# Entry of layer 0 of a two-layer diffusion backbone: unsplit modulation products, squares summed on TensorE, other weight order, two projections begun on half the features

## The chip, the cores and the metric

The kernel runs on one core of a Trainium2 chip. The core has five engines with queues of their own: TensorE (PE in the profile, its weight loads PEld), VectorE (DVE), ScalarE (ACT), GpSimd (POOL) and SyncE (SP), whose queue issues most transfers. TensorE reads on-chip memory (SBUF) and writes accumulators (PSUM). The metric is the device time of one execution in microseconds (us), as the median over runs.

## The reference, cut to what matters

One step of a two-layer backbone on 640 tokens (128 context, 512 latent) of 1024 features, all in 32-bit floats. Layer 0 runs gated linear attention beside latent attention, layer 1 differential attention; each is followed by a gated MLP. What the entry of layer 0 computes:

```python
s_ctx = silu(c_ctx)[None, :]; s_lat = silu(c)          # two conditioning vectors of 1024
mp = split(s_ctx @ w_ada[0] + b_ada[0], 6)             # context: shift, scale, gate, ...
ms = split(s_lat @ w_ada[0] + b_ada[0], 6)             # latent tokens
# rmsnorm(x, g) = x * rsqrt(mean(x * x) + 1e-6) * g ;  modulate(h, b, s) = h * (1 + s) + b
hp = modulate(rmsnorm(xp, norm_gain[0, 0]), mp[0], mp[1])
hs = modulate(rmsnorm(xs, norm_gain[0, 0]), ms[0], ms[1])
qa, ka, va, ga, lr_f, lr_b, cq, ckv, kr = split(h @ w_in)   # w_in: 1024 x 2144
```

## The kernel before

Activations lie with features on the 128 partitions (eight feature tiles, index k) and tokens along the rows, in two halves of 320 tokens (`CH`). To keep 32-bit accuracy with TensorE's faster format, an operand is split into a rounded part (hi, an ScalarE copy) and the rest (lo, a subtraction on VectorE or GpSimd), and three passes hi*hi, hi*lo, lo*hi stand for one product (`Weights.split`, lines 161 to 172; `proj`, lines 192 to 210). A product of unsplit 32-bit operands is issued as two slower passes.

The entry is lines 405 to 515. The two conditioning vectors go through SiLU (line 411). Of the modulation, only shift and scale of the first norm are needed at once: 2048 columns of `w_ada`, loaded as four groups of four quarters of 512 KB (line 419; quarters lie in turn in buffers `aw` and in the raw weight buffers `wraw`, four of each). `ada0(g)` multiplies group g: eight products, two per quarter, with the conditioning as the stationary operand of few columns and 512 columns of weights streaming. Quarter 1 of each group, and quarter 3 of group 3, are split first (hi on ScalarE, lo on GpSimd); the other eleven quarters are unsplit. The result is copied (line 438), transposed by TensorE (line 441) and given its bias. Groups 0 and 1 serve feature tiles 0 to 3, groups 2 and 3 tiles 4 to 7. Products and transposes take their accumulators in turn from the same two buffers (tag "p1").

`rms` (line 227) makes the norm factors of one half: it squares the eight tiles (ScalarE, lines 235 and 238), adds them up (VectorE, line 239), lets TensorE add over the partitions with a matrix of -1 (line 242) and takes the inverse root in a chain of ScalarE and VectorE steps (lines 244 to 250). The factors stay in a PSUM tile of tag "s". `apply_norm` (line 308) multiplies x by scale and factor (line 316), adds the shift (ScalarE, line 318) and splits into hi and lo: even tiles on VectorE (line 320), odd ones with a copy on ScalarE and a subtraction on GpSimd (lines 177 and 178). After groups 0 and 1 it runs tiles 0 to 3 of half 0, then of half 1; after groups 2 and 3 likewise tiles 4 to 7.

`ein(i)` loads, splits and multiplies block i of the input projection: 48 passes of 320 columns into one "s" tile. The blocks come in the order 0, 9, 10, 11, 12, 5, 6, 7, 8, 1, 2, 3, 4. Block 0 carries the low-rank decays, from which the decay products (`zmm`, line 504) are made right after block 9. Beside the blocks, VectorE works off the rest of the modulation of layer 0 as reductions against the conditioning (`Ada`, line 375, loads `araw`); these wait for the SiLU of line 479.

"s" tiles lie in two buffers, and each third one in a third buffer (`Ps.__call__`). In the entry the first two hold the factors of the halves, the third is block 0's and the fourth, in the buffer of the first, block 9's.

The order on each engine is not that of the text: a planner simulates the program with its own costs and places instructions by text order and readiness; after that each engine's queue runs strictly in the planned order. `tc.issue_after(i)` puts what is issued inside behind instruction i, but only on i's own engine.

Of the kernel before, what the change touches and what calls it, by code (L numbers as in the profile page):

```python
# [19 lines left out]
D = 1024  # L20
KT = 8
# [35 lines left out]
def build(tc, a):  # L57
# [169 lines left out]
    def rms(tp, bank, parts, denom, out=None, y=None, after=None, bufs=1):  # L227
# [7 lines left out]
        S.activation(out=acc, in_=parts[0], func=ACTF.Square)  # L235
        for s in parts[1:]:
            sq = sq_tile()
            S.activation(out=sq, in_=s, func=ACTF.Square)
            V.tensor_tensor(out=acc, in0=acc, in1=sq, op=ALU.add)  # L239
        o, q, y = bank[:, 0:n], sq_tile(), acc if y is None else y  # L240
        with tc.issue_after(after.ins) if after else ExitStack():
            PE.matmul(out=o, lhsT=negs, rhs=acc, start=True, stop=True)
# [65 lines left out]
    def apply_norm(tp, x, bc, hl, l, n, half, k0=0, k1=KT):  # L308
        c0, c1 = CH[half]
        for k in range(k0, k1):  # L310
            t = tp.tile([128, CUT], FP32, tag="nm_t", name="nm_t", bufs=3)[:, 0:c1 - c0]
            hi, lo = [z[:, k, c0:c1] for z in hl]
            for s0, s1, c in seg(c0, c1):
# [4 lines left out]
                S.activation(out=u if k % 2 else hi[:, r], in_=u, func=ACTF.Identity, bias=sh)  # L318
# [89 lines left out]
    csil = xp.tile([128, KT, 4], FP32, name="csil")  # L408
    csr = xp.tile([128, KT, 4], FP32R, name="csr")
    V.memset(csil, 0.0)  # L410
    tables(S.activation(out=csil[:, :, 0:2], in_=sm["cT"], func=ACTF.Silu))
    split(csil[:, :, 0:2], csr[:, :, 0:2], csr[:, :, 2:4])

    awp, awes = pool("aw", side="left")
    raws = []
    for g in range(4):
        for q in range(4):
            raws.append(W.tile("raw", [128, 2, 512], FP32) if q % 2 else awp.tile([128, 2, 512], FP32, tag="aw", name="aw", bufs=4))
            load = nc.sync.dma_start(out=raws[-1], in_=a["wada0a"][g, q])
        if g == 0:  # L420
            for q in range(4):
                nc.sync.dma_start(out=x[:, 2 * q:2 * q + 2], in_=a["xT"][:, 2 * q:2 * q + 2])

    def ada0(g):
        am = ps("p1", "adaps")
        for q in range(4):
            raw = raws[4 * g + q]
            if q % 2 == 0 or q == 3 and g < 3:
                for kk in range(2):
                    PE.matmul(out=am[0:4, :], lhsT=csil[:, 2 * q + kk], rhs=raw[:, kk], start=q == 0 and kk == 0, stop=q == 3 and kk == 1)  # L430
                continue
            w = W.split(raw, [128, 2, 512], G)
            for kk in range(2):
                k = 2 * q + kk
                PE.matmul(out=am[0:4, :], lhsT=csr[:, k], rhs=w[0][:, kk], start=False, stop=False)
# [932 lines left out]
```

## Time and profile before

| | |
|---|---|
| runs | 1793.81, 1790.93, 1793.09 us; median 1793.09 |
| profiled execution | 1789.83 us, span of its instructions 1788.1 us |
| TensorE busy | 1730.6 us (97%) |
| VectorE, ScalarE, GpSimd busy | 1256.9, 757.4, 310.0 us |
| mean granted TensorE clock | 0.989 of full speed |
| read from main memory | 166.59 MB |

Times in the rows are counted from the start of the span. The profile is of one execution, the median is over three others. TensorE's passes overlap, so a reported pass is longer than the distance to the next one, and the pace is read from starts. "<-" behind a wait names what ended it, as the profile infers it.

### The profile page before, as it was taken

What the parts mean: (1) busy time and instruction counts of PE and PEld (TensorE: products, weight loads), DVE (VectorE), ACT (ScalarE), POOL (GpSimd) and SP (SyncE); (2) the same over time, 40 slices, a digit from 0 to 9 for tenths busy, and PEclk for the clock granted to TensorE, in tenths of its full rate; (3) what the DMA queues carried; (4) which work ended last, traced back from release to release, by engine and by line L of the source; (5) the groups of instructions that cost most, each with busy time, mean ns of one, the idle gap of its engine ahead of it and who ended that gap; (6) DMA issues with size and microseconds to landing.
All of it is one profiled execution on the core that took longest, in us unless ns stands there. A gap on an engine that the chain in (4) does not pass through costs nothing. (4 is left out here: it accounts for less than half of the span.)

```text
span 1788.1 us, 29411 instructions
## 1 busy us (share of the span) xinstructions
PE 1730.6 (97%) x11716; PEld 1622.1 (91%) x11716; DVE 1256.9 (70%) x2398; ACT 757.4 (42%) x1354; POOL 310.0 (17%) x330
## 2 busy tenths in 40 slices
PE   6999999999999999999989999999999999999997
PEld 1898777889999999999988989898999999999996
DVE  4974877778799999945587777876575454545556
ACT  5454535544522232322366665665363232323233
POOL 3201021000310100000124243431041010101004
PEclk9999999999999999999999999998999999999998
DMA  9650002054356555522232111212122222222221
GB/s 359 211 178 10 29 1 74 4 186 133 95 177 200 166 178 179 163 65 89 63 117 73 34 59 36 72 50 72 59 83 83 71 79 75 71 83 71 60 83 60
DMA packets 57337, 176.59 MB, mean 99 GB/s; under 512 B 6064, under 2 KB 11568, under 8 KB 56816
## 3 DMA queue, kind: packets, MB, share of 16 engines
q1 hardware_dynamic: 53408, 160.59, 27.9%
q0 software_dynamic: 3792, 14.13, 2.3%
q8 instruction: 92, 1.51, 0.3%
q14 instruction: 45, 0.37, 0.1%
HBM read 166.59 MB, written 7.77 MB: 98 GB/s over the span
## 5 line engine op out<-in xcount | busy, mean ns | idle before, releaser
L207 PE MATMUL up<-B,whi 128*128 128x320 f32 x2560 | 479.2, 309 | 0.0
L163 ACT CAST whi<-wraw 128x1024 fp32r<-128x1024 f32 (+2 forms) x208 | 208.1, 1001 | 520.2 <-PE up L207 232.0
L207 PEld LDWEIGHTS up<-B,whi 128*128 128x128 f32 x2560 | 401.7, 188 | 0.0
L170 DVE TENSOR_TENSOR wlo<-wraw,whi 128x1024 fp32r<-128x1024 f32 (+2 forms) x175 | 205.0, 1172 | 226.5 <-ACT whi L163 226.5
L207 PE MATMUL up<-B,wlo 128*128 128x320 f32 x1280 | 291.4, 309 | 0.0
L207 PE MATMUL po<-A,whi 128*128 128x320 f32 x1312 | 246.3, 309 | 0.7 <-DVE u L980 0.5
L207 PEld LDWEIGHTS up<-B,wlo 128*128 128x128 f32 x1280 | 214.1, 188 | 0.0
L375 DVE CUSTOM_DVE_ANT_0 junk<-araw,cbc 128x1024 bf16<-128x1024 f32 x160 | 204.6, 1279 | 10.2 <-DMA araw<-in_wada0b 8.2
L178 POOL TENSOR_TENSOR A<-u,A 128x640 fp32r<-128x640 f32 x44 | 76.6, 1741 | 754.9 <-ACT A L177 729.9
L207 PEld LDWEIGHTS po<-A,whi 128*128 128x128 f32 x1312 | 205.8, 188 | 1.4 <-issue 0.7
L207 PE MATMUL po<-A,wlo 128*128 128x320 f32 x656 | 149.8, 309 | 0.5 <-DVE wlo L170 0.5
L216 PE MATMUL qko<-B,whi 128*128 128x320 f32 x512 | 118.6, 316 | 4.6 <-ACT B L318 1.6
L170 POOL TENSOR_TENSOR wlo<-wraw,whi 128x256 fp32r<-128x256 f32 (+1 forms) x117 | 97.5, 862 | 132.6 <-ACT whi L163 127.2
L352 PE MATMUL pot<-A,whi 128*128 128x320 f32 x512 | 114.0, 311 | 0.1
L207 PEld LDWEIGHTS po<-A,wlo 128*128 128x128 f32 x656 | 109.8, 188 | 0.8 <-DVE wlo L170 0.8
L978 DVE SCALAR_TENSOR_TENSOR u<-up,small,u 128x127 f32<-128x127 f32 (+1 forms) x176 | 95.5, 542 | 8.2 <-ACT u L976 7.4
L980 DVE SCALAR_TENSOR_TENSOR u<-up,small,u 128x127 f32<-128x127 f32 (+1 forms) x176 | 96.2, 548 | 4.5
L216 PEld LDWEIGHTS qko<-B,whi 128*128 128x128 f32 x512 | 86.7, 191 | 6.9 <-ACT B L318 1.9
L865 ACT ACTIVATE p<-sc,mn 128x768 f32<-128x768 f32 (+1 forms) x100 | 79.2, 796 | 31.2 <-DVE mn L864 30.5
L864 DVE TENSOR_REDUCE mn<-sc 128x1 f32<-128x768 f32 (+1 forms) x100 | 79.2, 816 | 13.7 <-PE sc L839 13.4
L352 PEld LDWEIGHTS pot<-A,whi 128*128 128x128 f32 x512 | 85.6, 188 | 1.4 <-issue 0.4
L334 DVE SCALAR_TENSOR_TENSOR x2t<-po,mod,x2t 128x128 f32<-128x128 f32 x88 | 44.2, 546 | 55.3 <-PE po L207 50.6
(296 smaller groups left out, 3048.7 us busy)
## 6 DMA issues: line engine op xcount, KB each, us to landing
wraw<-in_wup SPq DMA_DIRECT2D x88, 512.0 KB, 3.6
araw<-in_wada SPq DMA_DIRECT2D x48, 512.0 KB, 3.5
wraw<-in_wdn SPq DMA_DIRECT2D x40, 512.0 KB, 3.7
araw<-in_wada0b SPq DMA_DIRECT2D x32, 512.0 KB, 4.1
wraw<-in_wie SPq DMA_DIRECT2D x13, 512.0 KB, 4.3
aw<-in_wada0a SPq DMA_DIRECT2D x8, 512.0 KB, 9.3
wraw<-in_wada0a SPq DMA_DIRECT2D x8, 512.0 KB, 8.9
wraw<-in_woe SPq DMA_DIRECT2D x8, 512.0 KB, 4.3
```

What stands on the lines that cost most here:

```text
L163: S.copy(out=hi, in_=raw)
L170: eng.tensor_tensor(out=lo[:, z], in0=raw[:, z], in1=hi[:, z].bitcast(FP32), op=ALU.subtract)
L178: return (lo_eng or V).tensor_tensor(out=lo, in0=src, in1=hi.bitcast(FP32), op=ALU.subtract)
L207: PE.matmul(out=o, lhsT=w[wi][:, k], rhs=hl[ri][:, k, c0:c1], start=k == 0 and n == 0, stop=k == nk - 1 and n == 2)
L216: PE.matmul(out=o, lhsT=w[wi][:, k], rhs=hl[ri][:, k, c0:c1], start=k == 0 and n == 0, stop=k == nk - 1 and n == 2)
L334: V.scalar_tensor_tensor(out=x[:, k, s0:s1], in0=ps_ap[:, s0 - c0:s1 - c0], scalar=mods[l][:, g * KT + k, c:c + 1], in1=x[:, k, s0:s1], op ...
L352: PE.matmul(out=o, lhsT=ws[j + m][wi][:, k], rhs=hl[ri][:, k, c0:c1], start=k == 0 and n == 0, stop=k == nk - 1 and n == 2)
L375: V.tensor_tensor_reduce(out=junk, in0=raw, in1=self.cbc[:, j], op0=ALU.mult, op1=ALU.add, scale=1.0, scalar=0.0, accum_out=mods[l][:, t0 ...
L864: V.tensor_reduce(out=mn[:, m:m + 1], in_=ss[m][:, 0:nk], op=ALU.min, axis=AX.X)
L865: self.exp = S.activation(out=p[:, m, 0:nk], in_=ss[m][:, 0:nk], func=ACTF.Exp, scale=-1.0, bias=mn[:, m:m + 1], accum_out=li[:, m:m + 1])
L978: V.scalar_tensor_tensor(out=u[:, s0 + 1:s1], in0=r[:, s0:s1 - 1], scalar=cw[:, 0:1], in1=u[:, s0 + 1:s1], op0=ALU.mult, op1=ALU.add)
L980: last = V.scalar_tensor_tensor(out=u[:, s0:s1 - 1], in0=r[:, s0 + 1:s1], scalar=cw[:, 2:3], in1=u[:, s0:s1 - 1], op0=ALU.mult, op1=ALU.add)
```

## The change

All sixteen modulation quarters are multiplied unsplit, two columns of conditioning wide, and the zeroed and split copies of the conditioning go. `rms` gets a form (`pe=True`) in which TensorE sums the eight squared tiles itself, one product each; both halves' factors share one "s" tile. Groups 1 to 3 are queued on TensorE behind the last of these sums. The norm takes half 0 and half 1 of one feature tile together. The raw weights of block 0 are loaded ahead of group 3, those of blocks 9 and 10 behind it and ahead of the rotary tables and the conditioning. Blocks 0 and 9 are issued first for tiles 0 to 3, both, then for tiles 4 to 7 (`ein_part`). The SiLU of line 479 is queued on ScalarE behind the last step of the norm there.

```diff
--- before.py
+++ after.py
@@ -224,7 +224,7 @@
         with tc.issue_after(after.ins) if after else ExitStack():
             mark["tab"] = S.preload_act_table_set("natural_log_exp_and_others")
 
-    def rms(tp, bank, parts, denom, out=None, y=None, after=None, bufs=1):
+    def rms(tp, bank, parts, denom, out=None, y=None, after=None, bufs=1, pe=False):
 
         n = parts[0].shape[-1]
 
@@ -232,14 +232,18 @@
             return tp.tile([128, CUT], FP32, tag="rsq", name="rsq", bufs=2)[:, 0:n]
 
         acc = tp.tile([128, CUT], FP32, tag="racc", name="racc", bufs=bufs)[:, 0:n]
-        S.activation(out=acc, in_=parts[0], func=ACTF.Square)
-        for s in parts[1:]:
-            sq = sq_tile()
+        o = bank[:, 0:n]
+        for k, s in enumerate(parts):
+            sq = sq_tile() if k or pe else acc
             S.activation(out=sq, in_=s, func=ACTF.Square)
-            V.tensor_tensor(out=acc, in0=acc, in1=sq, op=ALU.add)
-        o, q, y = bank[:, 0:n], sq_tile(), acc if y is None else y
-        with tc.issue_after(after.ins) if after else ExitStack():
-            PE.matmul(out=o, lhsT=negs, rhs=acc, start=True, stop=True)
+            if pe:
+                mark["sum"] = PE.matmul(out=o, lhsT=negs, rhs=sq, start=k == 0, stop=k == len(parts) - 1)
+            elif k:
+                V.tensor_tensor(out=acc, in0=acc, in1=sq, op=ALU.add)
+        q, y = sq_tile(), acc if y is None else y
+        if not pe:
+            with tc.issue_after(after.ins) if after else ExitStack():
+                PE.matmul(out=o, lhsT=negs, rhs=acc, start=True, stop=True)
         with tc.issue_after(mark["tab"].ins):
             S.activation(out=q, in_=o, func=ACTF.Ln, scale=-1.0 / denom, bias=epst[:, 0:1])
             S.activation(out=y, in_=q, func=ACTF.Exp, scale=-0.5, bias=lnh[:, 0:1])
@@ -306,7 +310,7 @@
                          scale=gs[l][:, n, k, c:c + 1], bias=mods[l][:, 3 * n * KT + k, c:c + 1])
 
     def apply_norm(tp, x, bc, hl, l, n, half, k0=0, k1=KT):
-        c0, c1 = CH[half]
+        last, (c0, c1) = None, CH[half]
         for k in range(k0, k1):
             t = tp.tile([128, CUT], FP32, tag="nm_t", name="nm_t", bufs=3)[:, 0:c1 - c0]
             hi, lo = [z[:, k, c0:c1] for z in hl]
@@ -315,7 +319,7 @@
                 u, sh = t[:, r], mods[l][:, 3 * n * KT + k, c:c + 1]
                 V.scalar_tensor_tensor(out=u, in0=x[:, k, s0:s1], scalar=gs[l][:, n, k, c:c + 1], in1=bc[:, r],
                                        op0=ALU.mult, op1=ALU.mult)
-                S.activation(out=u if k % 2 else hi[:, r], in_=u, func=ACTF.Identity, bias=sh)
+                mark["norm"] = S.activation(out=u if k % 2 else hi[:, r], in_=u, func=ACTF.Identity, bias=sh)
                 if k % 2 == 0:
                     last = V.scalar_tensor_tensor(out=lo[:, r], in0=u, scalar=sh, in1=hi[:, r].bitcast(FP32),
                                                   op0=ALU.add, op1=ALU.subtract)
@@ -405,55 +409,49 @@
     misc = gg.tile([128, TOK], FP32, name="misc")
     xp, xes = pool("x0", side="right")
     x = xp.tile([128, KT, TOK], FP32, name="x0t")
-    csil = xp.tile([128, KT, 4], FP32, name="csil")
-    csr = xp.tile([128, KT, 4], FP32R, name="csr")
-    V.memset(csil, 0.0)
-    tables(S.activation(out=csil[:, :, 0:2], in_=sm["cT"], func=ACTF.Silu))
-    split(csil[:, :, 0:2], csr[:, :, 0:2], csr[:, :, 2:4])
+    csil = xp.tile([128, KT, 2], FP32, name="csil")
+    tables(S.activation(out=csil, in_=sm["cT"], func=ACTF.Silu))
 
     awp, awes = pool("aw", side="left")
-    raws = []
+    raws, pre = [], {}
     for g in range(4):
+        if g == 3:
+            pre[0] = W.raw(a["wie"][0], [128, KT, 128])
         for q in range(4):
             raws.append(W.tile("raw", [128, 2, 512], FP32) if q % 2 else awp.tile([128, 2, 512], FP32, tag="aw", name="aw", bufs=4))
-            load = nc.sync.dma_start(out=raws[-1], in_=a["wada0a"][g, q])
+            nc.sync.dma_start(out=raws[-1], in_=a["wada0a"][g, q])
         if g == 0:
             for q in range(4):
                 nc.sync.dma_start(out=x[:, 2 * q:2 * q + 2], in_=a["xT"][:, 2 * q:2 * q + 2])
+    for i in (9, 10):
+        pre[i] = W.raw(a["wie"][i], [128, KT, 128])
+    load = W.last_dma
 
     def ada0(g):
         am = ps("p1", "adaps")
         for q in range(4):
-            raw = raws[4 * g + q]
-            if q % 2 == 0 or q == 3 and g < 3:
-                for kk in range(2):
-                    PE.matmul(out=am[0:4, :], lhsT=csil[:, 2 * q + kk], rhs=raw[:, kk], start=q == 0 and kk == 0, stop=q == 3 and kk == 1)
-                continue
-            w = W.split(raw, [128, 2, 512], G)
             for kk in range(2):
-                k = 2 * q + kk
-                PE.matmul(out=am[0:4, :], lhsT=csr[:, k], rhs=w[0][:, kk], start=False, stop=False)
-                PE.matmul(out=am[0:2, :], lhsT=csr[:, k, 0:2], rhs=w[1][:, kk], start=False, stop=k == KT - 1)
-        ar = xp.tile([4, 512], FP32, tag="ar", name="ar", bufs=2)
-        V.tensor_copy(out=ar, in_=am[0:4, :])
+                PE.matmul(out=am[0:2, :], lhsT=csil[:, 2 * q + kk], rhs=raws[4 * g + q][:, kk], start=q == 0 and kk == 0, stop=q == 3 and kk == 1)
+        ar = xp.tile([2, 512], FP32, tag="ar", name="ar", bufs=2)
+        V.tensor_copy(out=ar, in_=am[0:2, :])
         at = ps("p1", "adat")
         for b in range(4):
-            PE.transpose(out=at[:, 4 * b:4 * b + 4], in_=ar[:, b * 128:(b + 1) * 128], identity=ident[0:4, 0:4])
+            PE.transpose(out=at[:, 2 * b:2 * b + 2], in_=ar[:, b * 128:(b + 1) * 128], identity=ident[0:2, 0:2])
         t0 = (g % 2) * 8 + (g // 2) * 4
-        av = at[:, 0:16].rearrange("p (t c) -> p t c", c=4)
-        add_b(0, t0, 4, av[:, :, 0:2])
-        m = mods[0][:, t0:t0 + 4]
-        V.tensor_tensor(out=m, in0=m, in1=av[:, :, 2:4], op=ALU.add)
+        add_b(0, t0, 4, at[:, 0:8].rearrange("p (t c) -> p t c", c=2))
         if g % 2:
             make_g(0, 0, (g // 2) * 4, (g // 2) * 4 + 4)
 
     ada0(0)
-    bcs = [rms(xp, ps("s", "rb")[:, 0:512], [x[:, k, c0:c1] for k in range(KT)], D, bufs=2) for c0, c1 in CH]
+    rb, last = ps("s", "rb"), None
+    bcs = [rms(xp, rb[:, 512 * h:512 * h + 512], [x[:, k, c0:c1] for k in range(KT)], D, bufs=2, pe=True) for h, (c0, c1) in enumerate(CH)]
     for g in range(1, 4):
-        ada0(g)
+        with tc.issue_after(mark["sum"].ins):
+            ada0(g)
         if g % 2:
-            for half in range(2):
-                last = apply_norm(xp, x, bcs[half], B, 0, 0, half, 2 * (g - 1), 2 * (g - 1) + 4)
+            for k in range(2 * (g - 1), 2 * (g - 1) + 4):
+                for half in range(2):
+                    last = apply_norm(xp, x, bcs[half], B, 0, 0, half, k, k + 1) or last
     xes.close()
     awes.close()
     scp, sces = pool("sc", side="left")
@@ -475,7 +473,7 @@
     adp.after = [last, load]
     with tc.issue_after(load.ins):
         adp.load(a["cbc"])
-    with tc.issue_after(last.ins):
+    with tc.issue_after(mark["norm"].ins):
         S.activation(out=adp.cbc, in_=adp.cbc, func=ACTF.Silu)
     cbd = drp.tile([128, 2, D], FP32, name="cbd")
     nc.gpsimd.dma_start(out=cbd, in_=adp.cbc)
@@ -483,7 +481,23 @@
         adp.group(0, 16 + 8 * c, [a["wada0b"][8 * c + i] for i in range(8)])
 
     def ein(i):
-        return proj(ps("s", "pe"), W(a["wie"][i], [128, KT, 128]), B, KT)
+        if i in begun:
+            return ein_part(i, KT // 2, KT)
+        w = W.split(pre.pop(i), [128, KT, 128]) if i in pre else W(a["wie"][i], [128, KT, 128])
+        return proj(ps("s", "pe"), w, B, KT)
+
+    begun = {}
+
+    def ein_part(i, k0, k1):
+        if k0 == 0:
+            begun[i] = (ps("s", "pe"), W.split(pre.pop(i), [128, KT, 128]))
+        pt, w = begun[i]
+        for k in range(k0, k1):
+            for n, (wi, ri) in enumerate(((0, 0), (0, 1), (1, 0))):
+                for c0, c1 in CH:
+                    PE.matmul(out=pt[:, P0 + c0:P0 + c1], lhsT=w[wi][:, k], rhs=B[ri][:, k, c0:c1],
+                              start=k == 0 and n == 0, stop=k == KT - 1 and n == 2)
+        return pt[:, P0:P0 + TOK]
 
     def rope(tp, z, t0=0):
         n, t1 = z.shape[0], t0 + z.shape[-1]
@@ -505,6 +519,8 @@
                       rhs=wdec[d * 32:d * 32 + 32, :], start=True, stop=True)
         return z
 
+    for i in (0, 9):
+        ein_part(i, 0, KT // 2)
     S.activation(out=misc, in_=ein(0), func=ACTF.Identity, bias=sm["miscb"][:, 0:1])
     nc.gpsimd.dma_start(out=kr[:, TOK:ALLK], in_=a["krc"])
     nc.gpsimd.dma_start(out=kr[64:128, 0:TOK], in_=misc[64:128, :])
```

## Rows read from the trace of the kernel before

**Rows 1.** The page's first part: busy us (share of the span) and instructions of each engine.

```profile
PE 1730.6 (97%) x11716; PEld 1622.1 (91%) x11716; DVE 1256.9 (70%) x2398; ACT 757.4 (42%) x1354; POOL 310.0 (17%) x330
```

**Rows 2.** Windows: stretch, length, busy us (instructions) by engine, TensorE clock, DMA share, GB/s.

```profile
60.00:70.00 10.00, 10.00 (x69) 9.48 (x68) 8.28 (x12) 3.88 (x5) 2.88 (x6) 1.00 0.63 189
```

**Rows 3.** Groups by line, TensorE, 54.4 to 65.5: xcount | busy, mean ns | idle before.

```profile
L207 PE MATMUL pe<-B,whi 128*128 128x320 f32 x47 | 8.9, 311 | 2.1 <-DVE nm_t L316 2.1
L207 PE MATMUL pe<-B,wlo 128*128 128x320 f32 x24 | 5.5, 309 | 0.0
```

**Rows 4.** Timeline of TensorE: start, duration, line, operation, count [idle before, releaser].

```profile
5.61 3.57 PE L430 MATMUL adaps<-aw,csil 128*4 128x512 f32 x4 [5.61 <-DMA aw<-in_wada0a]
...
22.73 0.40 PE L436 MATMUL adaps<-wlo,csr 128*2 128x512 f32 x1 [1.86 <-POOL wlo L170]
...
35.32 1.88 PE L430 MATMUL adaps<-wraw,csil 128*4 128x512 f32 x4
...
38.30 1.88 PE L430 MATMUL adaps<-aw,csil 128*4 128x512 f32 x4
...
43.40 0.40 PE L435 MATMUL adaps<-whi,csr 128*4 128x512 f32 x1
43.63 0.40 PE L436 MATMUL adaps<-wlo,csr 128*2 128x512 f32 x1
...
54.49 0.85 PE L207 MATMUL pe<-B,whi 128*128 128x320 f32 x4 [2.14 <-DVE nm_t L316]
...
65.09 0.70 PE L504 MATMUL z<-wdec,misc 32*128 32x256 f32 x4
...
73.59 0.85 PE L207 MATMUL pe<-B,whi 128*128 128x320 f32 x4
```

**Rows 5.** Timeline of TensorE's weight loads, one ahead of each pass.

```profile
12.49 0.09 PEld L430 LDWEIGHTS adaps<-aw,csil 128*4 128x4 f32 x1 [0.34 <-issue]
12.92 0.09 PEld L430 LDWEIGHTS adaps<-aw,csil 128*4 128x4 f32 x1 [0.34 <-issue]
```

**Rows 6.** Line 242 over the whole kernel: count: least/median/greatest ns, first to last start.

```profile
L242 PE MATMUL rb<-racc,negs x32: 432/433/537, 19.8 to 1777.5; 128*128 128x320 f32 x32
```

**Rows 7.** Timeline of TensorE in a later stage, unsplit products of 256 columns.

```profile
190.47 1.13 PE L620 MATMUL inc<-va,kdt 128*128 128x256 f32 x4
```

**Rows 8.** Timeline of VectorE (DVE).

```profile
25.89 2.37 DVE L239 TENSOR_TENSOR racc<-racc,rsq 128x320 f32<-128x320 f32 x1 [0.45 <-ACT rsq L238]
...
28.18 0.67 DVE L438 COPY ar<-adaps 4x512 f32<-4x512 f32 x1
...
30.23 1.84 DVE L316 SCALAR_TENSOR_TENSOR nm_t<-x0t,gs,rb 128x128 f32<-128x128 f32 x6
...
39.63 0.50 DVE L248 SCALAR_TENSOR_TENSOR rb<-rb,rsq 128x320 f32<-128x320 f32 x1 [0.85 <-ACT rsq L247]
...
48.28 1.84 DVE L316 SCALAR_TENSOR_TENSOR nm_t<-x0t,gs,rb 128x128 f32<-128x128 f32 x6
...
66.67 1.22 DVE L170 TENSOR_TENSOR wlo<-wraw,whi 128x1024 fp32r<-128x1024 f32 x1
```

**Rows 9.** Timeline of GpSimd (POOL).

```profile
25.56 2.35 POOL L170 TENSOR_TENSOR wlo<-wraw,whi 128x1024 fp32r<-128x1024 f32 x1 [2.89 <-ACT whi L163]
...
58.87 1.37 POOL L178 TENSOR_TENSOR B<-nm_t,B 128x320 fp32r<-128x320 f32 x1 [1.08 <-ACT B L177]
```

**Rows 10.** Timeline of ScalarE (ACT).

```profile
37.97 0.53 ACT L244 ACTIVATE rsq<-rb,scal 128x320 f32<-128x320 f32 x1 [1.93 <-PE rb L242]
...
40.91 1.91 ACT L479 ACTIVATE cbc<-cbc 128x2048 f32<-128x2048 f32 x1
```

**Rows 11.** Windows of 2 us; the clock is the third number from the end.

```profile
32.00:34.00 2.00, 2.00 (x5) 0.34 (x4) 1.50 (x6) 2.00 (x6) 0.67 (x1) 0.57 0.99 410
...
48.00:50.00 2.00, 2.00 (x9) 2.00 (x9) 1.96 (x7) 1.56 (x6) 0.22 (x1) 0.50 0.74 227
```

**Rows 12.** Waits of the SP queue, 0 to 66: total us, times, longest.

```profile
SPq L155 <- DVE wlo L170: 8.7, 2, 7.3
```

## The prediction

> **What bounds the kernel now.** I read the page's busy times first: TensorE is busy 97% of the span [rows 1], so time can only come from stretches where it stands still, runs at its lower clock, or does work that need not be done. The windows of 10 us came next: from 60 us on it is busy without a gap [rows 2], so what the entry hands over earlier moves the whole rest forward, and nothing in the entry counts except the moment from which TensorE streams the projections without a break. The timeline of TensorE gives that moment. The projections of blocks 0 and 9 need 96 passes of 320 columns; the groups by line count 71 of them after 54.4 us [rows 3], and the decay products behind them start at 65.09 [rows 4]. 54.49 to 65.09 is 10.6 us for some 72 passes, 0.147 us each: full pace. So 24 passes, the first half of block 0, came before, and TensorE stood 2.14 us ahead of 54.49. The releaser is VectorE's line 316, and that is no operand: the accumulator of block 9 is the fourth "s" tile, which reuses the one in which the norm factors of half 0 lie, and line 316 is their last reader. The number to predict is what replaces 65.09.
>
> **The sum.** Start: TensorE begins at 5.61 and its first four passes take 3.57 [rows 4]; a pass of 512 columns later takes 0.43 [rows 5], so a full-precision product of 512 columns (two passes) costs 0.86.
>
> Group 0 unsplit: eight products. The first two run at the slow pace (3.4 us), six take 5.2: done at 14.2. Before, its split quarter waited for ScalarE's cast and POOL's subtraction.
>
> Sums of squares: sixteen products of 128x320 replace fourteen VectorE additions and two products. A pass of this line is reported as 433 ns [rows 6]; the 512-column pass is reported about 0.16 longer than its pace, so the pace here is 0.27, a sum 0.54. From below: two passes overlapped wholly, 0.43; from above: four passes of 256 columns in 1.13 with 0.40 for the last [rows 7] pace at 0.243, which scales to 0.61. I take 0.54, the line's own row: 8.6 us (6.9 to 9.8). The squares go through two buffers, and one is also held by the factor chain of half 0 for 2.2 us (Ln at 37.97 to the product that ends at 40.13, [rows 8, 10]); meanwhile half 1 has one buffer, and a sum costs a square (0.5, like the Ln there) and a product one after the other, 1.0, instead of 0.54. Loss 0 to 1.6; I take 0.7. With 0.3 for the transposes of group 0, the last sum ends at 23.8 (21.4 to 26.2).
>
> Groups 1 to 3 are queued behind that sum on TensorE alone: 24 products, 48 passes of 0.43, 20.6 us. Between groups TensorE waits for the copy of the result, because two buffers carry both the products and their transposes: the last four passes of group 2 start at 35.32, group 3 at 38.30, which less 1.72 of streaming is 1.26 us [rows 4]. Two such gaps, 2.5; of a third, in front of the projections, 0 to 1.26, I take 0.8, since the first halves do not need it. First halves start at 47.7. Before, the last product of group 3 started at 43.63: the groups end later, not earlier.
>
> First halves of blocks 0 and 9: 48 passes, 7.0 us, to 54.8. Their accumulators are free, since both halves' factors now share one "s" tile.
>
> The norm of the other features runs meanwhile. From copy to first product took 28.18 to 30.23, 2.0 us [rows 8], so it starts at 48.9. Before it took from 48.28 to the end of the last POOL subtraction, 60.24 [rows 8, 9], with two weight subtractions of 1.2 in VectorE's queue; those weights now come before it, so 9.5 us: ready at 58.4. TensorE wants that last operand at 47.7+7.0+3x0.88+0.4=57.8. Stall 0.6, bounds 0 and 3.
>
> Second halves: 7.0 us. End 47.7+14.1+0.6=62.4. Gain 65.1-62.4=2.7 us. Cross-check: five quarters unsplit add 5x(1.72-0.92)=4.0 us of TensorE work (split passes follow at 0.23, [rows 4]) and fourteen sums 7.6. This 11.6 is paid out of waiting, such as 1.86 us for POOL ahead of 22.73.
>
> Edits at nothing. The SiLU of the layer's conditioning (1.91 and a table load ahead of it, [rows 10]) stood between the factors and the norm of half 1; it goes behind the norm, where only the VectorE reductions follow, and they start no earlier than the norm's end either way. Uncovered it costs these 1.91 and the load on VectorE, not on TensorE: VectorE's weight part at 66.67 is for the block that TensorE begins at 73.59 [rows 4, 8], 5.7 us of slack after its 1.2. Fewer VectorE additions, a smaller copy and no zeroing shorten queues that had slack. The weight loads moved ahead of the SP queue: block 0's load takes the buffer of a group-1 quarter and waits for TensorE until about 27 (23.8 and two quarters); block 10's takes block 0's buffer and waits for VectorE's subtraction (SP has waited 8.7 us for that already, [rows 12]). Queued behind it: the rotary tables, the conditioning and the reductions' loads. None is wanted before 55; a wait up to 50 is free, beyond it VectorE's reductions slip into the same 5.7 us.
>
> **One rule against the change.** VectorE's addition at 25.89 took 2.37 us beside a POOL subtraction of 2.35, an operation of that size otherwise 0.5 [rows 8, 9]. The Trainium skill, page "SBUF — State Buffer", section "Who interferes with whom", says that VectorE and GpSimd share one port pair as an exclusive lock, so that one of them stands still. By that rule the four POOL parts of the second norm would each stop VectorE; the norm would last about 12 us and the gain would be near nothing. The trace agrees at 25.89. My 9.5 us come from a stretch with the same POOL work, so such stops are partly in it already.
>
> **Rivals.**
> Fully packed: the planner puts first halves into the gaps between the groups, the sums lose nothing to the buffers and nothing stalls: 23.1+20.6+14.1=57.8, or 60.3 with the two gaps kept; gain 4.8 to 7.3, 1785.8 to 1788.3. For: the operands of the first halves come from group 1, ready long before. Against: such gaps stayed empty before.
>
> Norm still decides: groups end near 47, 3 us later than before, and the norm takes 12 us again because the weights' subtractions stay inside it: ready at 60.9, then the last feature of block 0 and block 9's second half (4.4): 65.3, gain about 0: 1793. For: it took that long before, and SP's wait can delay those weights. Against: VectorE and ScalarE have less to do.
>
> Slower by the clock: TensorE's granted clock was half, 1.2 GHz, in 32 to 34 and all of 48 to 50 [rows 11], after short waits and modest work. Unsplit products feed two weight columns and now make up most of the entry. Every 2 us at that clock lose 1. From 5.4 us of it the gain is gone, from about 13 it is slower by 0.2%; all three groups at 1.2 GHz would cost 20.6, or 1811. A few such spells: 1795 to 1800. Against: such products held full pace in 12 to 15 [rows 5]. The Trainium skill, page "TensorE: Matmul & The Clock Gate", Part 1, says the clock falls after idleness and comes back with activity; by that rule less idleness means fewer falls; the trace shows full pace right after the 2.14 us of waiting ahead of 54.49 [rows 3, 4], so it does not bear the rule out there.
>
> **How the numbers follow.** The profiled execution took 1789.83, span 1788.1 and 1.7 around it; that less 2.7 is 1787.1. It lies 3.3 under the median of the runs, 1793.09, against which I predict 1790.4. Forecast (gain 1 to 4.5; alone 1788.6 to 1792.1) 0.42; fully packed 0.25; norm decides 0.17; slower 0.16. A measurement of this kernel tells 0.2%, 3.6 us, from no change: faster 0.25 plus 0.16 of the forecast, 0.41; slower 0.14 (two parts in a hundred of that rival fall within); same the rest, 0.45. The range goes from 1785.5, the packed case with a little of the sums' cheap end, to 1797.0: every unknown at its dear end (26.2+20.6+2.5+1.3+14.1+3=67.7, 2.6 later than now) with 2.6 us at the lower clock.
>
> **What would show it.** Right: no POOL work before the norm; group 3's last pass near 46; projections from about 47.5 without a break; decay products near 62.4. The sums are wrong if group 1 starts outside 21 to 26; the cover is wrong if TensorE waits for line 316, 320 or 178 between the halves; the hand-over is wrong if the decay products move and the span does not. A clock row of 0.5 over the groups is the slow rival. All is wrong if TensorE still waits for the factors' tile.

## The result: 15 us slower

The changed kernel took 1807.07 us (median of 4 runs, 1806.36 to 1809.43) against 1792.01 for the kernel before: ratio 1.0087, 95% interval 1.0068 to 1.0107. The profiled execution took 1807.1, its span 1805.2. The page's busy line, in the columns of [rows 1]:

```profile
PE 1747.8 (97%) x11744; PEld 1630.5 (90%) x11744; DVE 1244.2 (69%) x2378; ACT 753.5 (42%) x1348; POOL 296.8 (16%) x325
```

VectorE, ScalarE and GpSimd have less to do, as the change meant, and TensorE 17.2 us more. The loss has a place: the decay products, the hand-over of [rows 4], start at 78.80 instead of 65.09, 13.7 later. From there to the first product of the next stage it is 88.2 us instead of 86.6, another 1.6. These two make 15.3 of the 17.1 us between the two profiled spans; the medians, of other executions, lie 15.1 apart. TensorE's timeline of the changed kernel, in the columns of [rows 4], shows the 13.7:

```profile
6.07 3.57 PE L434 MATMUL adaps<-aw,csil 128*2 128x512 f32 x4 [6.07 <-DMA aw<-in_wada0a]
...
15.73 1.34 PE L240 MATMUL rb<-rsq,negs 128*128 128x320 f32 x4
...
17.34 4.07 PE L240 MATMUL rb<-rsq,negs 128*128 128x320 f32 x12
24.50 6.66 PE L240 MATMUL rb<-rsq,negs 128*128 128x320 f32 x16 [3.09 <-DVE rb L254]
31.09 1.88 PE L434 MATMUL adaps<-aw,csil 128*2 128x512 f32 x4
...
39.22 1.88 PE L434 MATMUL adaps<-aw,csil 128*2 128x512 f32 x4
...
46.18 0.85 PE L498 MATMUL pe<-B,whi 128*128 128x320 f32 x4
...
50.25 1.88 PE L434 MATMUL adaps<-aw,csil 128*2 128x512 f32 x4
...
57.21 0.71 PE L498 MATMUL pe<-B,whi 128*128 128x320 f32 x3
...
61.08 0.41 PE L439 MATMUL adat<-small,ar 2*128 2x2 f32 x4
63.13 2.03 PE L498 MATMUL pe<-B,whi 128*128 128x320 f32 x7 [1.31 <-ACT B L322]
...
72.77 1.26 PE L498 MATMUL pe<-B,whi 128*128 128x320 f32 x4 [1.83 <-ACT B L177]
...
78.80 0.70 PE L518 MATMUL z<-wdec,misc 32*128 32x256 f32 x4 [2.44 <-DMA wdec<-in_wdec]
```

Read from the top: half 0's sums (L240) begin at 15.73; half 1's wait 3.09 us and end at 31.09, where group 1 begins; block 0's first half fills the gap in front of group 3 (46.18), which then starts at 50.25; block 9's first half (57.21 on) stands ahead of group 3's transposes (61.08), without which the norm of the other features cannot begin; then come a wait for a cast of the norm and one for the decay weights. VectorE (the norm, and the modulation's reductions, which came at 58.28 before):

```profile
61.92 1.72 DVE L320 SCALAR_TENSOR_TENSOR nm_t<-x0t,gs,rb 128x128 f32<-128x128 f32 x5
...
72.40 1.23 DVE L379 CUSTOM_DVE_ANT_0 junk<-araw,cbc 128x1024 bf16<-128x1024 f32 x1 [3.85 <-ACT cbc L477]
```

ScalarE at the end of that norm; the SiLU of the conditioning and its table load run ahead of the last cast, for the edit put them behind the last Identity (L322), not behind the last cast (L177):

```profile
68.58 0.56 ACT L322 ACTIVATE nm_t<-nm_t,mod 128x320 f32<-128x320 f32 x1
69.16 1.28 ACT L477 ACT_TABLE_LOAD   x1
70.45 1.91 ACT L477 ACTIVATE cbc<-cbc 128x2048 f32<-128x2048 f32 x1
72.27 0.44 ACT L177 CAST B<-nm_t 128x320 fp32r<-128x320 f32 x1
```

GpSimd, whose queue also issues the decay weights; the copy of the SiLU's result (L479) stands ahead of the norm's last subtraction (L178), and both ahead of that load (L467):

```profile
72.67 0.56 POOL L479 DMA_DIRECT2D cbd<-cbc  x1 [3.08 <-ACT cbc L477]
73.26 1.09 POOL L178 TENSOR_TENSOR B<-nm_t,B 128x320 fp32r<-128x320 f32 x1
74.30 0.55 POOL L467 DMA_DIRECT2D wdec<-in_wdec  x1
```

The 1.6 us behind the hand-over are a spell at 1.2 GHz. TensorE's windows of the changed kernel (length, busy, granted clock, DMA share, GB/s):

```profile
80.00:82.00 2.00, 2.00 (x10) 0.50 1.01 249
82.00:84.00 2.00, 2.00 (x11) 0.69 1.01 368
```

Windows of the kernel before behind its own decay products (66 to 72) showed the full clock. Ahead of the hand-over the lower clock makes no difference between the two: windows of 5 us there (length times 1 - granted clock) add up to some 3.4 us lost in either kernel.

### The profile page after: what moved, and what is told of

The parts are those of the page before. It is cut to its first block, busy times and chain, and to the rows that moved or that the text cites. A ratio compares the mean times of both kernels' runs of the same rounds, so it can differ in the third digit from the quotient of the medians.

```text
span 1805.2 us, 29419 instructions
## 1 busy us (share of the span) xinstructions
PE 1747.8 (97%) x11744; PEld 1630.5 (90%) x11744; DVE 1244.2 (69%) x2378; ACT 753.5 (42%) x1348; POOL 296.8 (16%) x325
## 5 line engine op out<-in xcount | busy, mean ns | idle before, releaser
L163 ACT CAST whi<-wraw 128x1024 fp32r<-128x1024 f32 (+2 forms) x203 | 202.9, 1001 | 523.4 <-PE up L207 231.4
L178 POOL TENSOR_TENSOR A<-u,A 128x640 fp32r<-128x640 f32 x44 | 76.2, 1732 | 756.9 <-ACT A L177 731.9
L170 POOL TENSOR_TENSOR wlo<-wraw,whi 128x256 fp32r<-128x256 f32 x112 | 85.8, 797 | 106.0 <-ACT whi L163 106.0
L880 DVE TENSOR_REDUCE mn<-sc 128x1 f32<-128x768 f32 (+1 forms) x100 | 79.2, 816 | 15.5 <-PE sc L855 15.1
L338 DVE SCALAR_TENSOR_TENSOR x2t<-po,mod,x2t 128x128 f32<-128x128 f32 x88 | 44.2, 546 | 55.3 <-PE po L207 50.6
```

Source lines behind the costliest of these rows:

```text
L163: S.copy(out=hi, in_=raw)
L170: eng.tensor_tensor(out=lo[:, z], in0=raw[:, z], in1=hi[:, z].bitcast(FP32), op=ALU.subtract)
L178: return (lo_eng or V).tensor_tensor(out=lo, in0=src, in1=hi.bitcast(FP32), op=ALU.subtract)
L880: V.tensor_reduce(out=mn[:, m:m + 1], in_=ss[m][:, 0:nk], op=ALU.min, axis=AX.X)
```

## The experiments

"Hand-over" is the start of the first decay product in the profiled execution, which is one of the runs. The median of the kernel before was 1790.07 to 1791.2 beside e1 to e15, and ratios are against its runs on the same chip. The entry itself began earlier in the profiled executions of e1 to e5 and e10 than in the changed kernel's (first sum at 15.0, 14.1, 14.5, 14.2, 14.5 and 14.7 instead of 15.73, same instructions before it), so 0.7 to 1.6 us of a gain in hand-over are not the edit's.

| kernel | hand-over | median us (runs) | ratio (95%) |
|---|---|---|---|
| before | 65.1 | 1792.01 (4) | 1 |
| changed | 78.8 | 1807.07 (4) | 1.0087 (1.0068 to 1.0107) |
| e1 sums before chains | 72.9 | 1804.94 (4) | 1.0084 (1.0062 to 1.0106) |
| e2 transposes first | 73.4 | 1803.91 (4) | 1.0077 (1.0062 to 1.0092) |
| e3 SiLU last | 73.2 | 1800.15 (4) | 1.0058 (1.0043 to 1.0073) |
| e4 decay weights early | 74.7 | 1809.74 (4) | 1.0102 (1.0085 to 1.0119) |
| e5 all four | 66.1 | 1797.0 (10) | 1.0033 (1.0016 to 1.0050) |
| e6 e5, products split | 66.8 | 1800.58 (5) | 1.0050 (1.0032 to 1.0068) |
| e7 e2 to e4, VectorE sums | 61.2 | 1791.42 (10) | 1.0002 (0.9978 to 1.0025) |
| e8 e7, products split | 69.3 | 1799.05 (9) | 1.0035 (1.0016 to 1.0054) |
| e9 e7, SiLU in the norm | 62.6 | 1792.99 (12) | 1.0001 (0.9990 to 1.0012) |
| e10 changed, SiLU in the norm | 74.1 | 1803.53 (6) | 1.0063 (1.0047 to 1.0080) |
| e11 before, unsplit products | 65.6 | 1791.76 (11) | 0.9996 (0.9985 to 1.0007) |
| e12 changed, VectorE sums | 67.7 | 1798.75 (9) | 1.0039 (1.0026 to 1.0052) |
| e14 e9, block 0 first | 63.5 | 1792.3 (12) | 1.0004 (0.9990 to 1.0017) |
| e15 e14, weights late | 63.2 | 1790.89 (12) | 1.0006 (0.9991 to 1.0020) |

**One wait each.** Theory A: the loss is four waits that the order makes, each removable by order alone. Theory B: it is the added TensorE work.

e1 takes both halves' sums before either factor chain:

```diff
-    bcs = [rms(xp, rb[...], [...], D, bufs=2, pe=True) for h, (c0, c1) in enumerate(CH)]
+    for ph in ("sums", "chain"):      # rms does only its sums, or only its chain
+        bcs = [rms(xp, rb[...], [...], D, bufs=2, pe=ph) for h, (c0, c1) in enumerate(CH)]
```

> The changed kernel with one edit: the sums of squares of both halves are issued ahead of either half's factor chain, so that half 1's sums have no write of VectorE in the shared tile to wait for. Theory A (the loss is waits that the new order makes, each of which can be taken out by itself): the wait of 3.1 us for line 254 goes and the second eight sums run at about 0.6 us each; group 1 starts at 25 to 26.5 instead of 31.1, the decay products start near 73.5 instead of 78.8, time about 1802. Theory B (the loss is TensorE work added, 4.0 us of unsplit products and 7.6 of sums, and waits only sit where slack is left): group 1 starts earlier but the wait comes back in front of the second halves; decay products at 77.5 or later, time 1806 to 1808.

TensorE's timeline of e1:

```profile
16.62 9.54 PE L240 MATMUL rb<-rsq,negs 128*128 128x320 f32 x28
...
72.94 1.22 PE L521 MATMUL z<-wdec,misc 32*128 32x256 f32 x4 [2.50 <-DMA wdec<-in_wdec]
```

The wait is gone, group 1 starts at 26.1 instead of 31.1, the hand-over comes 5.9 earlier, 5.1 of it the edit's. The median fell by 2.1 only, less than either number of theory A. And 28 passes take 9.5 us, 0.34 each, at the full clock. ScalarE's timeline of e1 says why: two squares, then a wait for TensorE to free their two buffers, every 1.37 us.

```profile
20.19 1.01 ACT L238 ACTIVATE rsq<-x0t 128x320 f32<-128x320 f32 x2 [0.36 <-PE rb L240]
21.56 1.01 ACT L238 ACTIVATE rsq<-x0t 128x320 f32<-128x320 f32 x2 [0.35 <-PE rb L240]
```

e2 queues block 9's first half behind group 3's transposes:

```diff
-    for i in (0, 9):
-        ein_part(i, 0, KT // 2)
+    ein_part(0, 0, KT // 2)
+    with tc.issue_after(mark["adat"].ins):     # the last transpose
+        ein_part(9, 0, KT // 2)
```

> The changed kernel with one edit: the first half of block 9 is queued on TensorE behind the transposes of group 3. Theory A: the scale and shift of tiles 4 to 7 are ready 3.5 us earlier (norm starts near 58.3 instead of 61.9), the decay products start 3 to 3.7 us earlier, near 75.5, time about 1803.5. Theory B: the norm starts earlier but TensorE has the passes of block 9 still to do and ends no earlier than 78; time 1806 to 1808.

TensorE's timeline of e2: the last transposes come 5.2 earlier, 3.6 of it the edit's, the decay products 5.4 (3.7), though they now wait longer for their weights. That is theory A's outcome, and so is the median of 1803.91.

```profile
55.87 0.41 PE L439 MATMUL adat<-small,ar 2*128 2x2 f32 x4
...
73.45 0.77 PE L518 MATMUL z<-wdec,misc 32*128 32x256 f32 x4 [3.11 <-DMA wdec<-in_wdec]
```

e3 puts the SiLU behind the last cast:

```diff
-    with tc.issue_after(mark["norm"].ins):
+    with tc.issue_after(mark["cast"].ins):     # S.copy in split()
```

> The changed kernel with one edit: the SiLU of the conditioning is queued behind the last cast of the norm instead of behind its last shift. Theory A: the last cast runs at 69.1 instead of 72.3, the wait of 1.8 us for it goes, and the load of the decay weights behind it on the POOL queue moves too; decay products near 76, time about 1804. Theory B: no more than 1 us; time 1806 to 1808.

ScalarE's timeline of e3 has the order that was meant; the hand-over comes 5.6 earlier, 4.3 of it the edit's: more than theory A's 2.8 and than the 3.2 us of the SiLU and its load, since its copy on GpSimd's queue now stands behind the last subtraction and the decay weights too. The norm of tiles 4 to 7, first multiplication to last subtraction, takes 8.7 us instead of 12.4.

```profile
67.83 0.46 ACT L177 CAST B<-nm_t 128x320 fp32r<-128x320 f32 x1
68.31 1.28 ACT L477 ACT_TABLE_LOAD   x1
```

e4 issues the decay weights on SP's queue:

```diff
-    nc.gpsimd.dma_start(out=wdec, in_=a["wdec"])
     with tc.issue_after(load.ins):
+        nc.sync.dma_start(out=wdec, in_=a["wdec"])
```

> The changed kernel with one edit: the decay weights are loaded from the SP queue right behind the entry's loads, not from the POOL queue behind the norm's subtractions. Theory A: the wait of 2.4 us ahead of the decay products goes, they start at 76.4 instead of 78.8; time about 1804.5. Theory B: the wait moves to the next block, whose weight part VectorE subtracts at 76.6 to 77.8; time 1806 to 1808.

The hand-over comes 4.1 earlier (2.6 of it the edit's) and the total does not follow; it is past both theories. TensorE's waits in e4, 78 to 175 us (total, times, longest), show a new one, for the instruction with which VectorE reads decay products out of their accumulator (L544), while its reductions still begin late. From the hand-over to the next stage e4 needs 92.5 us, 4.3 more than the changed kernel.

```profile
PE pe L207 <- DVE ab L544: 3.4, 1, 3.4
```

e5 has all four edits.

> The changed kernel with the four edits together (sums of both halves first, block 9 behind group 3's transposes, SiLU behind the last cast, decay weights on SP's queue). Theory A (waits made by the order are the loss, and they add up): decay products near 63 to 65 instead of 78.8, as in the kernel before (65.1), time within 3 us of it. Theory C (TensorE's hand-over is no longer the bound: VectorE's reductions, which start behind the SiLU, now lag behind the blocks): decay products near 64 but a wait for VectorE later in the blocks gives back 3 to 6 us; time 1795 to 1798.

The four gains, 21.0 added up, are 15.8 without the earlier entry, and come to 11.4 together (12.7 less 1.3): they lay partly beside each other. The hand-over is back at 66.1, so B falls as an account of the whole 13.7: all the added work is still there. It is not back below 65.1 either, and the time (1797.0) is theory C's, not A's, though TensorE's only wait for VectorE's reading of decay products is gone.

**Which part costs what.** e6 splits the quarters again on top of e5; e7 takes e2 to e4 and lets VectorE add the squares again, without queueing the groups behind the sums; e8 is e7 with the quarters split.

```diff
-    bcs = [rms(xp, rb[...], [...], D, bufs=2, pe=True) for h, (c0, c1) in enumerate(CH)]
+    bcs = [rms(xp, rb[...], [...], D, bufs=2) for h, (c0, c1) in enumerate(CH)]
     for g in range(1, 4):
-        with tc.issue_after(mark["sum"].ins):
-            ada0(g)
+        ada0(g)
```

> The four repairs, and the five modulation quarters split again as in the kernel before. Theory D (with the waits out, what is left is TensorE work, and unsplit products cost 4.0 us of it): decay products 3 to 4 us earlier than with the four repairs alone. Rival (the splits bring back their own waits for ScalarE and POOL, 1.6 to 1.9 us each): within 1 us of it.

> The repairs that apply, with the squares added up by VectorE again and the groups no longer queued behind the sums; products stay unsplit. Theory D: fourteen sums less on TensorE are worth 7 to 9 us; decay products 55 to 58 unless the norm of tiles 4 to 7 binds at about 60. Rival: VectorE's additions delay the copies and the factors, decay products within 2 us of those of the four repairs.

> Split products and VectorE's sums as in the kernel before, with the rest of the change (shared factor tile, weight order, halves of blocks 0 and 9) and the repairs that apply. Theory D: least TensorE work of the four kernels, decay products at 56 to 60, time 1783 to 1788 if nothing behind binds. Rival (theory C): decay products there, but VectorE's reductions bind behind them, time 1788 to 1793.

VectorE's sums are worth 4.9 us of hand-over and 5.6 of the median (e5 to e7), less than theory D's 7 to 9. So theory B holds for a part: with the four waits gone, some 5 us of the loss are left, and they go when TensorE no longer makes the sums. Splitting the quarters again saves nothing, against theory D: it costs 0.7 (e5 to e6) or 8.1 (e7 to e8), the latter where VectorE has the sums as well; for e8 theory D had forecast the earliest hand-over of all, and its rival too. TensorE's timelines of e7, then e8, show where these two part, at the product that completes half 1's sum (L246):

```profile
27.36 0.81 PE L246 MATMUL rb<-racc,negs 128*128 128x320 f32 x2 [0.79 <-DVE racc L242]
```

```profile
37.60 0.81 PE L246 MATMUL rb<-racc,negs 128*128 128x320 f32 x2
```

In e8 it stands behind group 2's split products, though VectorE's last addition ended at 30.4; the norm of tiles 4 to 7 then ends at 65.3 instead of 57.2. In e7's profiled execution, a long one of 1802.67 us, the lead of 3.9 is lost before the next stage, at a wait for VectorE and to the lower clock (5.1 us); TensorE's timeline of e7:

```profile
61.18 1.13 PE L517 MATMUL z<-wdec,misc 32*128 32x256 f32 x4 [2.13 <-ACT misc L524]
...
120.99 1.44 PE L207 MATMUL pe<-B,whi 128*128 128x320 f32 x4 [3.27 <-DVE ab L544]
```

e9 is e7 with the SiLU's own edit undone, e10 the changed kernel with that alone undone, e11 the kernel before with unsplit quarters alone, e12 the changed kernel with VectorE's sums alone (the diff shown for e7).

```diff
-    with tc.issue_after(mark["norm"].ins):     # e7: mark["cast"]
+    with tc.issue_after(last.ins):
```

> The kernel of e7 (VectorE's sums, unsplit products, block 9's half behind the transposes, the decay weights early), but the SiLU of the conditioning stands where it stood before, between the norm factors and the norm of the second half. Theory C (VectorE's reductions bind behind the hand-over because the late SiLU lets them begin late): decay products at 61 to 63, the reductions begin before 59 and end near 118 instead of 124.8, TensorE's 3.3 us for VectorE's ab is gone, 1784 to 1788. Theory D (the reductions are held by their own loads, 11.0 us of idle time in e7): an early SiLU doesn't help, the wait for ab stays, the SiLU and its table load cost up to 3.2 us in the norm, decay products at 63 to 65, 1792 to 1796.

> The changed kernel with one edit undone: the SiLU of the conditioning back between the norm factors and the second half of the norm. Theory A (the moved SiLU delayed the last casts and, over its copy to memory, POOL's queue with the decay weights): both waits go, decay products from 78.8 to 72 to 74, some 1799 to 1801. Theory B (its 1.9 us and the table load then stand in the norm, which sets the end here): decay products at 75 to 77, 1802 to 1805.

> The kernel before with one part of the change alone: the five split quarters of the modulation products are unsplit. Theory A (the split's casts and subtractions held VectorE, POOL and TensorE more than the 4.0 us of added TensorE work): the wait of 1.86 us for POOL ahead of group 1 goes and the norm's engines are freer, decay products at 62 to 64, 1787 to 1789.5. Theory B (added passes stand in front of the groups, and the block 9 accumulator still waits for the norm's last reader): decay products at 64.5 to 66, 1790 to 1793.

> The changed kernel with one edit undone: the squares are summed on VectorE again, and groups 1 to 3 are not queued behind the sums. Theory A (the sums on TensorE cost their passes and the wait of 3.1 us for half 0's factors): the hand-over comes 5 to 8 us earlier, 70.8 to 74, some 1799 to 1802. Theory B (the norm's end with its late casts and the decay weights sets the hand-over in any case): it moves by less than 3 us, 76 to 78.8, 1804 to 1807.

e9: the reductions begin at 55.3 and end at 116.6, and the wait for VectorE at 120.99 is gone, so theory C holds for it; but the median did not reach 1788, so C's time failed. e10: 4.7 us of hand-over (3.7 of it the edit's) and 3.5 of the median, which is theory B's time, and of A's two waits the one for the decay weights stayed (2.28): their load stands behind the norm's last subtraction on GpSimd whatever the SiLU does. It stood there before, too, issued 4.9 us ahead of the decay products; there 4 us of passes behind the norm hid it, and the early first halves took these away. e11's hand-over and time are theory B's, and the norm's last reader of the factors' tile still releases block 9, as in [rows 4]. But theory A's part is in it as well: the waits for GpSimd are gone, TensorE's waits ahead of the decay products sum to 13.1 us instead of 17.1, and block 9 begins 2.2 earlier; a spell at 1.2 GHz right behind takes that back in this execution (0.94 at 58 to 60 again). TensorE's timeline and windows of e11:

```profile
52.26 1.43 PE L207 MATMUL pe<-B,whi 128*128 128x320 f32 x4 [1.70 <-DVE nm_t L316]
```

```profile
54.00:56.00 2.00, 2.00 (x9) 0.50 0.00 0
56.00:58.00 2.00, 2.00 (x9) 0.50 0.00 0
```

e12 is the largest single step: 11.1 us of hand-over (group 0 was done up to 1.9 earlier, not by the edit), 8.3 of the median, past theory A's 5 to 8. Of the hand-over 4.1 are given back before the next stage (92.3 us to it instead of 88.2), 2.8 of them to the lower clock. TensorE's timeline of e12:

```profile
67.68 1.22 PE L517 MATMUL z<-wdec,misc 32*128 32x256 f32 x4 [2.53 <-DMA wdec<-in_wdec]
```

**What is lost behind the hand-over.** e14 queues block 9's second half behind block 0's last pass, so that block 0's eviction is covered; e15 does so with the decay weights on GpSimd's queue, as in the change.

```diff
         if i in begun:
-            return ein_part(i, KT // 2, KT)
+            with tc.issue_after(mark["ein"].ins):   # the last pass issued for a block
+                return ein_part(i, KT // 2, KT)
```

> The kernel of e9 with the second half of block 9 queued behind the last pass of block 0, so that block 0's eviction lies beside block 9's passes, as it did before. Theory E (the 1.7 us that every variant loses between the decay products and the next stage is a spell at half the clock, which follows the wait of 2.4 us ahead of the decay products): the wait shrinks under 0.8 us, there is no window at 0.50 behind it, decay products at 61 to 63, the next stage's length is that of before, and the total is 1785 to 1789. Theory F (the 1.7 us is work or order that the change added behind the hand-over): the stage stays 1.6 to 1.7 longer whatever the wait does, 1789 to 1793.

> As e14, but the decay weights stay on POOL's queue as in the changed kernel. If their lateness there came only from the moved SiLU (the copy of its result stands ahead of them), they land in time and this equals e14 within 0.1%. If POOL's own norm work delays them, the decay products wait for them 1 to 3 us, a spell at half the clock follows, and it is 2 to 4 us slower than e14.

Theory E's mechanism holds; its hand-over (61 to 63) and its total (1785 to 1789) do not, and the total is F's. e9's timeline and TensorE's windows, then e14's:

```profile
62.59 1.16 PE L517 MATMUL z<-wdec,misc 32*128 32x256 f32 x4 [2.38 <-DVE wlo L170]
```

```profile
64.00:66.00 2.00, 2.00 (x9) 0.50 1.02 270
```

```profile
63.52 0.70 PE L518 MATMUL z<-wdec,misc 32*128 32x256 f32 x4
```

```profile
64.00:66.00 2.00, 2.00 (x15) 1.00 0.99 293
```

With the wait the stretch from the decay products to the next stage is 1.7 longer than before, without it (e14, e15) the same within 0.1. e15 equals e14 with the decay weights behind GpSimd's last subtraction, since block 9's passes stand behind block 0's last and hide the load again, as in the kernel before.

Both lead the kernel before by 2.4 and 2.8 us at 406 us, and in their totals the lead cannot be seen. In their profiled executions what swallows it lies in layer 1's attention, 900 to 1270 us: summed over windows of 10 us, length times (1 - granted clock), that stretch lost 11.9 us in the kernel before, 18.7 in e14 and 13.7 in e15. Yet the order of TensorE's instructions from the next stage on is the same in e14 and e15, one by one. TensorE's windows of the same work, e14 and then e15:

```profile
1052.00:1056.00 4.00, 4.00 (x16) 0.54 0.43 135
```

```profile
1052.00:1056.00 4.00, 4.00 (x27) 1.00 0.48 135
```

So the same order of work can meet a spell there or not. Executions of one kernel scatter by it: of the kernel before's 25 beside e5, those with a mean clock of 0.988 or 0.989 took 1787.5 to 1791.1, those with 0.983 to 0.985 took 1795.7 to 1797.5.

Such spells are not why e5's median stays 6 above that of before with a hand-over only 1.0 later, though 17.1 us were lost there in its profiled execution. At a mean clock of 0.988 or 0.989 e5's executions took 1794.1 to 1795.8, some 5 us more than the kernel before at the same clock, and its mean loss over ten executions (span times 1 - mean clock) was 24.3 us against 23.0. In its profiled execution e5 was only 1.7 later at 406 us; a part of the rest is a wait for VectorE in the same attention stage, which in the kernel before is 0.6 at most. TensorE's waits of e5, 1030 to 1150 us:

```profile
PE pv L916 <- DVE pt L183: 2.0, 1, 2.0
```

What else makes these 5 us stays open. For e14 and e15 the same reckoning gives 24.3 and 23.9 us against 22.3: more spells than before, but not clear of the scatter. Whether some orders draw more of them than others stays open; no version was shown to beat the kernel before.

## Why the prediction was wrong

The forecast was 1790.4, in 1785.5 to 1797.0; 1807.07 lies outside, on the side that had 0.14. What it took as the number to predict was right for this change: hand-over and total moved together, 13.7 and 15.1. It is not the whole: in e4, e7, e14 and e15 the hand-over came earlier and the total did not follow. The failure is in the working of 62.4, against 78.8:

| step | predicted | measured | off by |
|---|---|---|---|
| group 0 done | 14.2 | 15.7 (e1 to e4: 14.1 to 15.0) | 1.5 |
| last sum ends | 23.8 (21.4 to 26.2) | 31.1 | 5.8 more |
| groups 1 to 3 done, from there | 23.1 | 26.0 | 2.9 |
| from there to the norm's start | 2.0 | 4.8 | 2.8 |
| norm of tiles 4 to 7 | 9.5 | 12.4 | 2.9 |
| rest, to the decay products | 4.0 | 4.5 | 0.5 |

**The sums** are the failed step that costs most. The shared tile was counted only as a buffer freed for block 9. It also ties the halves: half 1's first square was ready at 22.3, and TensorE waited until 24.50, when VectorE had written half 0's factor (L254) into the same tile. The prediction gave half 1 a loss of 0 to 1.6 for one missing buffer; the wait alone is 3.09 (0.9 of it until the square was ready, 2.2 for the tile), and e1 removes it by order. The pace was mis-sized too: 0.54 a sum came from TensorE's own row, but two buffers tie squares and products to each other, at 1.37 us for two sums (e1), 0.68 each, some 2 us in sixteen. And after the wait the clock fell (windows 24 to 30 at 0.80, 0.50 and 0.85), some 1.7 us more.

**The first halves** were placed behind all groups at 47.7. The planner put block 0's in front of group 3 (2.9 us net of the gap) and block 9's in front of its transposes: the rival that was called fully packed, with the gap of 1.26 filled by 3.7 us of passes. The forecast said that the first halves do not need those transposes, and missed who does: the norm, which sets the end. Work that fills a gap is free only if nothing behind it in the queue is on the path; e2 measures this.

**The SiLU "at nothing"** failed. It was said to stand behind the norm. It stood behind the last Identity, ahead of the last cast, so its 1.28 + 1.91 fell into the norm (1.83 us of TensorE's waiting): less these 3.2 the norm took 9.2, near the 9.5 of the forecast, and 8.7 in e3. In the same way its copy stood ahead of the last subtraction and the decay weights on GpSimd's queue, which the prediction did not follow; the load, with only 2 us of passes left to hide it, was 2.44 late. Its other cover was VectorE's 5.7 us of slack: reductions that began 14 us later than before kept that slack only because the hand-over was late too; e4 and e7, with an earlier hand-over, wait 3.4 and 3.3 us for VectorE.

**What held.** The unsplit products alone change nothing (e11, 65.6 against 65.1, medians 0.6 apart): 4.0 us of work were paid out of waiting, which fell by 4.0. TensorE no longer waits for the factors' tile between the halves. The gap of 1.26 between groups is there again (31.09 to 39.22, less 6.87). "Norm still decides" was the nearest rival: norm of about 12 us, ready late; but it started from groups that end at 47 and so came to no loss.

**The two rules.** VectorE's line 320 ran at its usual pace beside GpSimd's subtraction of 64.87 to 65.74 (four instructions in 1.71 us from 64.61; the 320-column one among them 0.54 us, as at 68.00 with GpSimd idle), so the norm's 12.4 us do not come from such stops. The Trainium skill, page "SBUF — State Buffer", section "Who interferes with whom", excepts from the stop a VectorE instruction with at most one SBUF input (outside its two-port modes). Line 320 reads `x` from SBUF and the factor from PSUM; the addition at 25.89 in [rows 8] reads two SBUF tiles. So the trace agrees with the page in both places, and the prediction held the rule against instructions that it excepts.

The slow rival named the wrong cause: the groups ran at the full clock. The clock fell after waits: 24.50 (window 26 to 28 at 0.50), 72.77 (74 to 76 at 0.50), 78.80 (80 to 82), and not where the wait was ordered away (e14). The Trainium skill, page "TensorE: Matmul & The Clock Gate", Part 1, says that idleness brings the lower clock; most of the waits of 2 us and more agree, and the prediction was wrong to set the rule aside for one wait of 2.14 us that had no fall behind it. A second such wait is e6's, 2.14 us ahead of its decay products at 66.79.

## What to carry to other kernels

Where an engine's queue is strict, an operand's readiness is half the question: for each moved or added instruction ask what stands behind it in its queue and whether that is on the path (a transpose, a cast, a small load). Moving sums to the engine that bounds the kernel pays only if the producer's buffers keep its pace, and putting two independent chains into one accumulator tile can make them wait for each other. Cost a wait of 2 us and more on TensorE at its length and, as an estimate from these runs, up to 1.7 us for the clock behind it. Compare executions at the same mean clock before you blame the clock for a difference.

## What the runs showed of the hardware

A wait of 2.1 to 2.5 us just ahead of the decay products was followed, in the changed kernel, e5, e7 and e9, by a spell at 1.2 GHz that began 0.1 to 1.9 us after work resumed and cost 1.6 to 1.7 us; in e6, after 2.14 us, there was none, and for the same work without the wait (e14, e15) none either. The same TensorE order met such spells in one profiled execution and not in another, worth 5 us over 370 (e14 and e15); the executions of the kernel before spread over 10 us with their mean clock. That is more than most of the edits here.

A VectorE addition of two SBUF tiles took 2.37 us beside a GpSimd subtraction, 0.5 otherwise; a VectorE multiplication with one operand in PSUM took its usual 0.54 us beside one.
